# Two layers of a hybrid flow-matching block on one core: a new order for the first products, the sums of squares and the background modulation

## The chip, the cores and the metric

One core of one Trainium2 chip runs the whole program; times are device microseconds (us). A kernel is run several times and the median is compared. Engines in the text: PE is TensorE (matmuls), PEld its weight loads, DVE is VectorE, ACT is ScalarE, POOL is GpSimd, SP is SyncE, on whose queue all the DMAs named here are issued.

## The reference

512 latent tokens and 256 context tokens of width 1024 go through two layers, each a half-step SwiGLU, a mixer, and a second half-step SwiGLU; in each of the three the normalised input is scaled and shifted by a learned modulation of a conditioning vector. Cut to what matters here:

```
mod = (silu(c) @ w_mod[l] + b_mod[l]).reshape(c.shape[0], N_MOD, 1, D_MODEL)     # 9 blocks of 1024 columns
h = rms_norm(x, norm_g[l, 0]) * (1.0 + mod[:, 1]) + mod[:, 0]                     # scale and shift
u = h @ w_in
x = x + 0.5 * mod[:, 2] * ((silu(u[..., :D_FF]) * u[..., D_FF:]) @ w_out)         # D_FF = 2816
...
return rms_norm(x, final_norm_g)
```

The context tokens take the same path with their own modulation vector. The last layer's second SwiGLU has the latent tokens alone.

## The kernel before, in words

Everything is kept transposed in SBUF, as eight tiles `xT[k]` of 128 features by 768 tokens. The four feed-forward passes (`ffn`) loop over 22 steps `ff` of 128 columns of D_FF. A step is one call of `up`, which computes both up-projections of 128 columns by seven half-size products in place of eight (`EVEN1`, `T1`, `T2`, `ODD1`, `T3`, `ODD2`, `T4`). Each product is 4 pairs of feature tiles times 3 matmuls (both operands are split into a high and a low part), 12 matmuls in all, and accumulates in one of three PSUM banks `b`, `c`, `a` (tile name `ul`). The activations of the seven products are the tiles `bh`/`bl` (`self.B`), made on ACT and DVE by `pair_even` and by the generator `pair_odd`; the weights are `w1h`/`w1l`. `EVEN1` goes to `b`, is copied to `p1`, and `T2` and `T4` then add to the same bank; `T1` goes to `c`, is copied to `p5`, and `ODD2` adds to it. After `up` come the multiplication by the row's reciprocal root mean square (`rsb`), silu and gate (tiles `u`, `sg`, then `gh`/`gl`), and every two or three steps a chunk of down-projection (`mm3`, tile `y`), which DVE adds to `xT` (L595).

The RMS normalisation is applied behind the products. Its sums of squares are made by `sumsq(k)`: ACT squares a tile (`sq`), and six PE matmuls of one column each (`ssps`) add it up over the partitions. `raw_rows` turns the sums into reciprocal roots (`ssc`, 12 small DVE instructions) and spreads them over the partitions by six matmuls into two PSUM banks (`rst`).

The modulation is 18 blocks of 512 columns a layer. `mod_direct` and `mod_some` multiply the silu of the conditioning by weights (`wm`, eight loads of 256 KB for a block), `mod_rows` copies the sums (`mrow`) and transposes them by small matmuls (`modpt`) into `mod`. At the head, blocks 8 and 12 (scales of the first pass) and 0 and 4 (its shifts) are made directly. The shifts enter the products as two more columns of the activations (`raw_shifts`); the first `up` is computed without these columns, and a separate product (`bias`, L1102) adds them. The other blocks are made in the background of three `ffn` passes, by halves of four matmuls: 28 halves in the first pass, 12 in the second, 24 in the third. In each step `mod_some` does one half, or two in a row while more halves than steps are left, and loads the next half's four weights behind each.

A planner orders the instructions of each engine by a priority, which is the order of the program shifted by `high_priority(offset)`; a negative offset puts a block that many instructions later. What isn't ready by the planner's clock is passed over. Buffers of one tag are a ring. Tags that matter here:

```
PSUM "u", 7 banks: xps, modps (mod_direct), ul, rst, y, fps     PSUM "ms", 1 bank: modps (mod_some), modpt, ssps, bias
"t3", 2 buffers: sq, mrow, u                                    "wm", 4 buffers: weights of a half
"pc", 4 buffers: p1, p5, u2 (copies of ul), four x2 at the head "wo", 1 buffer: x3, wm6 (six weights of blocks 0 and 4), wb, wo
```

In the first pass `first_mods` makes the scales, the activations for `EVEN1` and then all eight sums of squares with offset -150; `first_shifts`, called behind the first `up`, loads and makes blocks 0 and 4 and the shifts. In the last pass `fin_tile(n)` squares, sums and transposes (`fps`) the finished tile of `xT` directly behind its down-projection, and `finish` normalises and stores.

Of the kernel before, what the change touches and what calls it, by code (L numbers as in the profile page):

```python
# [18 lines left out]
F32 = mybir.dt.float32  # L19
# [9 lines left out]
KT = 8  # L29
# [15 lines left out]
LATER = 300  # L45
SOON = 20
REST = 100
LATE0, LATE4, SQ0, SQ1 = 0, 0, 150, 150
NWQ, NW1, NPC = 6, 4, 4


# [71 lines left out]
class Whole:  # L123
# [103 lines left out]
            for k, r in enumerate(self.mod_w):  # L227
                self.nc.sync.dma_start(out=r, in_=self.a["w_mod"][l, (4 * h + k) * 128:(4 * h + k + 1) * 128, b * 128:b * 128 + 512])

    def mod_some(self, left):  # L230

        nc = self.nc
        for _ in range(2 if len(self.mod_todo) + 1 > left else 1):
            if self.mod_now is None:
                return
            l, b, h = self.mod_now
            if h == 0:
                self.mod_ps = self.psum("modps", "ms")
            for k, r in enumerate(self.mod_w):
                with self.tc.high_priority(offset=k):  # L240
                    nc.tensor.matmul(self.mod_ps[32 * k:32 * k + 32, :], lhsT=self.sc[:, 4 * h + k, :], rhs=r, start=h == 0, stop=h == 1,
                                     skip_group_check=True)
            if h == 1:
                self.mod_rows(l, b, self.mod_ps)
            self.mod_load()

    def scales(self, l, n, v):

# [163 lines left out]
    def ready(self, l, n, segs=SEGS, tag="ms"):  # L412

        def cb(k):
            if k == 0:
                self.raw_open(l, n, segs)
                self.held, self.rest = [], []
            with self.tc.high_priority(offset=-SQ1):
                self.sumsq(k, segs, tag)
            if n == 1:  # L420
                self.raw_tile(k)
                return
            m = k // 2
            if k % 2 == 0:
                self.held.append([self.half_tile() for _ in range(3)])
                self.pair_even(m, segs, self.held[m][0])
                return
            e2, o2, t = self.held[m]
            self.rest.append(self.pair_odd(m, segs, e2, o2, t))
            for _ in range(3):  # L430
                next(self.rest[m])
            if k == KT - 1:
                for i in range(3):
                    with self.tc.high_priority(offset=-REST - 15 * i):
                        for c in self.rest:
                            next(c)
        return cb
# [49 lines left out]
    def up(self, l, i, ff, first):  # L487


        nc, H = self.nc, self.half  # L490
        W = H + 2
        b, c, a = [self.psum("ul", "u") for _ in range(3)]
        ops = self.w1_operands(*(self.first_w1 if first else self.w1_load(l, i, ff)))
        z = 2 if first else 0
        keep = lambda: self.fw.tile([128, W], F32, name="pc", tag="pc", bufs=NPC)

        def product(n, out, start):
            wh, wl = next(ops)
            if first and n != EVEN1:
                for r in self.rest:  # L500
                    next(r, None)
            xh, xl = self.B[n]
            x0 = z if n in SHIFTED else 0
            for m in range(KT // 2):
                for j, (w, x) in enumerate(((wh, xh), (wh, xl), (wl, xh))):
                    nc.tensor.matmul(out, lhsT=w[:, m, :], rhs=x[:, m, x0:], start=start and m == j == 0, stop=m == KT // 2 - 1 and j == 2,  # L506
                                     skip_group_check=True)

        t = self.work.tile([128, 2 * H + 2], F32, name="u2", tag="t3")
        g = self.fw.tile([128, 2 * H], F32, name="sg", tag="sg", bufs=1)  # L510
        add = lambda out, x, y: nc.vector.tensor_tensor(out=out, in0=x, in1=y, op=ALU.add)
        product(EVEN1, b[:, z:W], True)
        p1 = keep()
        nc.scalar.copy(p1[:, z:W], b[:, z:W])
        product(T1, c[:, :H], True)
        p5 = keep()
        nc.scalar.copy(p5[:, :H], c[:, :H])
        product(T2, b[:, z:W], False)
        u2 = keep()
        nc.scalar.copy(u2[:, :H], b[:, 2:W])  # L520
        product(ODD1, a[:, z:W], True)
        add(t[:, z:W], a[:, z:W], p1[:, z:W])
        product(T3, b[:, 2:W], False)
        add(g[:, H:], b[:, 2:W], p5[:, :H])
        product(ODD2, c[:, :H], False)
        add(t[:, W:], c[:, :H], u2[:, :H])
        product(T4, b[:, z:W], False)
        return t, g, b

    def ffn(self, l, i, segs, chunks, background, last_cb, switch):  # L530
        nc, a = self.nc, self.a
        w2 = a["ffn_w_out"]
        H = self.half
        self.mod_todo = [(*t, h) for t in background for h in range(2)]
        f = 0
        for ci, cn in enumerate(chunks):
            gs = []
            for j in range(cn):
# [29 lines left out]
                gs.append((gh, gl))  # L568
                with self.tc.high_priority(offset=-LATER):
                    if ff:  # L570
                        self.mod_some(DFF // 128 - ff)
                    else:
                        self.mod_load()

# [13 lines left out]
            for n_ in range(KT):  # L588
                wh, wl = self.split(wo[:, :, n_ * 128:(n_ + 1) * 128], [128, cn, 128], "w2")
                py = [self.psum("y", "u")[:, :n] for o, n in segs]  # L590
                for j in range(cn):
                    self.mm3(py, wh[:, j, :], wl[:, j, :], gs[j][0], gs[j][1], segs, j == 0, j == cn - 1)
                for s, (o, n) in enumerate(segs):
                    xs = self.xT[n_][:, o:o + n]
                    nc.vector.scalar_tensor_tensor(out=xs, in0=py[s], scalar=gt[s][:, n_:n_ + 1], in1=xs, op0=ALU.mult, op1=ALU.add)  # L595
                if ci == len(chunks) - 1:
                    last_cb(n_)
            f += cn

    def gates(self, l, n, segs, half):  # L600
# [459 lines left out]
    def first_mods(self):  # L1060

        nc = self.nc
        ring = lambda pool, tag, n, bufs: [pool.tile([128, 512], F32, name="wm", tag=tag, bufs=bufs) for _ in range(n)]
        for b in (8, 12):
            self.mod_direct(0, b, self.mod_pieces(0, b, ring(self.hl, "w1h", 4, NW1) + ring(self.hl, "w1l", 4, NW1)))
        self.first_w1 = self.w1_load(0, 0, 0)
        self.raw_open(0, 0, shifts=False)
        self.rest = []
        for m in range(KT // 2):
            x2 = self.hl.tile([128, 2, self.half], F32, name="x2", tag=("gh", "gl")[m % 2], bufs=3)  # L1070
            t = self.fw.tile([128, self.half], F32, name="x2", tag="pc", bufs=NPC)
            self.pair_even(m, SEGS, x2[:, 0, :])
            self.rest.append(self.pair_odd(m, SEGS, x2[:, 0, :], x2[:, 1, :], t))
        for c in self.rest:
            next(c)
        with self.tc.high_priority(offset=-SQ0):
            for k in range(KT):
                self.sumsq(k)
            self.raw_rows(self.fw)

    def first_shifts(self):
        nc = self.nc
        ring = lambda pool, tag, n, bufs: [pool.tile([128, 512], F32, name="wm", tag=tag, bufs=bufs) for _ in range(n)]
        for b, late in ((0, LATE0), (4, LATE4)):
            w = self.raw.tile([128, 6, 512], F32, name="wm6", tag="wo", bufs=1)
            bufs = self.mod_pieces(0, b, [w[:, i, :] for i in range(6)] + ring(self.raw, "wm", 2, 4))
            with self.tc.high_priority(offset=-late):
                self.mod_direct(0, b, bufs, late)
        with self.tc.high_priority(offset=-LATE4 - 10):
            self.raw_shifts(0, 0)  # L1090

            w = self.raw.tile([128, KT, 256], F32, name="wb", tag="wo", bufs=1)
            for u in range(2):
                nc.sync.dma_start(out=w[:, :, 128 * u:128 * u + 128],
                                  in_=self.a["ffn_w_in"][0, 0, :, (1 - u) * DFF:(1 - u) * DFF + 128].rearrange("(k p) n -> p k n", p=128))
            sh = self.fw.tile([128, KT, 2], F32, name="sh0", bufs=1)
            for v in range(2):
                nc.vector.tensor_copy(sh[:, :, v], self.mod[0][v][:, :KT])
            pt = self.psum("bias", "ms")
            for u in range(2):  # L1100
                for k in range(KT):
                    nc.tensor.matmul(pt[:, 2 * u:2 * u + 2], lhsT=w[:, k, 128 * u:128 * u + 128], rhs=sh[:, k, :], start=k == 0, stop=k == KT - 1)  # L1102
            self.bias0 = self.fw.tile([128, 2, 2], F32, name="bias0", bufs=1)
            nc.vector.tensor_copy(self.bias0, pt[:, :4].rearrange("p (u v) -> p u v", u=2))
# [593 lines left out]
```

## Time and profile before

| | us |
|---|---|
| median of 3 runs | 3576.63 (3576.49, 3576.63, 3597.42) |
| profiled execution: its time | 3586.14 |
| profiled execution: its span | 3584.3 |
| PE busy / DVE busy / ACT busy in the span | 3417.7 / 2365.4 / 1533.6 |

The span is the profiled execution from its first to its last instruction; 1.8 us of its time lie around it. A busy PE is one that has a matmul in flight, which says nothing of how fast the matmul is.

### The profile page before, as it was taken

The numbers are of one execution on the slowest core, as the hardware profiler recorded it, in microseconds if no ns is written. First come the engines' busy times: TensorE is split into PE (matmuls) and PEld (weight loads), VectorE is DVE, ScalarE is ACT, GpSimd is POOL, SyncE is SP. The second block draws the span as 40 slices with busy tenths as digits, with TensorE's granted clock in tenths as the row PEclk, the third lists the DMA queues.
The fourth block names the chain that finished last, engine by engine and source line by source line (L and its number), as shares of the span: only waits on it lengthen the run. The fifth ranks groups of instructions, "written<-read, shape, count | busy, mean of one in ns | idle before, by whom it ended". The sixth has DMA issues, their size and how long they took to land. (4 is left out here: it accounts for less than half of the span.)

```text
span 3584.3 us, 60380 instructions
## 1 busy us (share of the span) xinstructions
PE 3417.7 (95%) x23736; PEld 2892.2 (81%) x23736; DVE 2365.4 (66%) x5210; ACT 1533.6 (43%) x3342; POOL 163.9 (5%) x342
## 2 busy tenths in 40 slices
PE   6899999999998999999999999999999989999997
PEld 5787898877776666998999879898888776678996
DVE  4566666545547875676777766666555567878885
ACT  4333333322446653433444424333333557644543
POOL 0000000000003230000000000000000022300000
PEclk7999999999999998999999899999999979999998
DMA  4434323211100002233221333323222100032331
GB/s 156 130 105 127 110 91 118 71 48 43 48 14 1 11 13 80 81 95 121 89 69 53 92 103 104 113 91 118 71 59 55 30 8 11 19 94 88 107 104 50
DMA packets 332941, 267.75 MB, mean 75 GB/s; under 512 B 33748, under 2 KB 281712, under 8 KB 332656
## 3 DMA queue, kind: packets, MB, share of 16 engines
q1 hardware_dynamic: 332656, 263.89, 24.0%
q8 instruction: 187, 3.06, 0.4%
q14 instruction: 98, 0.80, 0.1%
HBM read 261.72 MB, written 2.10 MB: 74 GB/s over the span
## 5 line engine op out<-in xcount | busy, mean ns | idle before, releaser
L506 PE MATMUL ul<-bh,w1h 128*128 128x386 f32 (+3 forms) x2464 | 807.5, 328 | 11.0 <-ACT w1h L455 4.1
L506 PE MATMUL ul<-bh,w1l 128*128 128x386 f32 (+3 forms) x2464 | 800.4, 326 | 2.0 <-DVE w1l L456 2.0
L506 PE MATMUL ul<-bl,w1h 128*128 128x386 f32 (+3 forms) x2464 | 802.1, 326 | 0.0
L455 ACT ACTIVATE w1h<-w1r 128x512 fp32r<-128x512 f32 x528 | 328.3, 631 | 499.8 <-PE ul L506 435.3
L506 PEld LDWEIGHTS ul<-bh,w1h 128*128 128x128 f32 x2464 | 467.9, 190 | 39.0 <-issue 15.4
L456 DVE TENSOR_TENSOR w1l<-w1r,w1h 128x512 fp32r<-128x512 f32 x528 | 359.8, 688 | 187.2 <-ACT w1h L455 182.6
L506 PEld LDWEIGHTS ul<-bl,w1h 128*128 128x128 f32 x2464 | 468.8, 190 | 4.6 <-issue 2.5
L506 PEld LDWEIGHTS ul<-bh,w1l 128*128 128x128 f32 x2464 | 467.2, 190 | 2.7 <-DVE w1l L456 2.5
L595 DVE SCALAR_TENSOR_TENSOR xT<-y,gate,xT 128x512 f32<-128x512 f32 x448 | 267.0, 632 | 209.3 <-PE y L447 207.3
L443 PE MATMUL y<-gh,w2h 128*128 128x512 f32 (+1 forms) x1232 | 348.6, 351 | 6.9 <-ACT gh L566 6.9
L445 PE MATMUL y<-gl,w2h 128*128 128x512 f32 (+1 forms) x1232 | 349.6, 349 | 0.3 <-DVE gl L567 0.2
L447 PE MATMUL y<-gh,w2l 128*128 128x512 f32 (+1 forms) x1232 | 347.2, 348 | 0.5 <-DVE w2l L456 0.4
L455 ACT ACTIVATE w2h<-wo 128x384 fp32r<-128x384 f32 (+1 forms) x256 | 124.7, 495 | 339.8 <-PE y L445 300.3
L443 PE MATMUL pj<-hh,pwh 128*128 128x512 f32 (+2 forms) x864 | 254.5, 348 | 1.8 <-DVE qA L1127 1.8
L447 PE MATMUL pj<-hh,pwl 128*128 128x512 f32 (+2 forms) x864 | 245.9, 342 | 1.2 <-DVE pwl L456 1.2
L445 PE MATMUL pj<-hl,pwh 128*128 128x512 f32 (+2 forms) x864 | 246.6, 342 | 0.0
L443 PEld LDWEIGHTS y<-gh,w2h 128*128 128x128 f32 x1232 | 198.9, 189 | 48.5 <-ACT gh L566 12.7
L447 PEld LDWEIGHTS y<-gh,w2l 128*128 128x128 f32 x1232 | 198.3, 190 | 37.1 <-issue 4.2
L445 PEld LDWEIGHTS y<-gl,w2h 128*128 128x128 f32 x1232 | 199.6, 190 | 32.9 <-DVE gl L567 2.3
L443 PEld LDWEIGHTS pj<-hh,pwh 128*128 128x128 f32 x864 | 150.2, 196 | 27.5 <-issue 7.9
L447 PEld LDWEIGHTS pj<-hh,pwl 128*128 128x128 f32 x864 | 146.7, 195 | 19.6 <-issue 5.1
L445 PEld LDWEIGHTS pj<-hl,pwh 128*128 128x128 f32 x864 | 147.7, 196 | 18.1 <-issue 7.6
(375 smaller groups left out, 5226.2 us busy)
## 6 DMA issues: line engine op xcount, KB each, us to landing
w1r<-in_ffn_w_in_dram SPq DMA_DIRECT2D x352, 256.0 KB
wm<-in_w_mod_dram SPq DMA_DIRECT2D x288, 256.0 KB
wo<-in_ffn_w_out_dram SPq DMA_DIRECT2D x88, 512.0 KB
pw<-in_w_in_dram SPq DMA_DIRECT2D x46, 512.0 KB
pw<-in_w_in_dram SPq DMA_DIRECT2D x16, 256.0 KB
wo<-in_w_out_dram SPq DMA_DIRECT2D x128, 32.0 KB
wo<-in_w_out_dram SPq DMA_DIRECT2D x64, 64.0 KB
rtab<-in_k_rope_dram SPq DMA_DIRECT2D x4, 512.0 KB
```

Of the source, the lines that this page charges most:

```text
L443: nc.tensor.matmul(p, lhsT=wh, rhs=xh[:, o:o + n], start=first, stop=False)
L445: nc.tensor.matmul(p, lhsT=wh, rhs=xl[:, o:o + n], start=False, stop=False)
L447: nc.tensor.matmul(p, lhsT=wl, rhs=xh[:, o:o + n], start=False, stop=last)
L455: nc.scalar.activation(out=hi, in_=raw, func=AF.Copy)
L456: nc.vector.tensor_tensor(out=lo, in0=raw, in1=hi, op=ALU.subtract)
L506: nc.tensor.matmul(out, lhsT=w[:, m, :], rhs=x[:, m, x0:], start=start and m == j == 0, stop=m == KT // 2 - 1 and j == 2, skip_group_check ...
L595: nc.vector.scalar_tensor_tensor(out=xs, in0=py[s], scalar=gt[s][:, n_:n_ + 1], in1=xs, op0=ALU.mult, op1=ALU.add)
```

## The change

At the head, the sums of squares leave `first_mods`. They are now called inside the first `up`: tiles 0 to 3 ahead of product `T3`, tiles 4 to 7 ahead of `ODD2`, and `raw_rows` ahead of `T4`, all without an offset. Modulation block 0 is computed ahead of `T1` and block 4 ahead of `ODD1`; the loads of block 0 stand behind those of the first step's weights. `first_shifts` keeps the shifts and the bias, 20 instructions later than its place. In the `ffn` passes `mod_some` does one half only, and a second half is done inside `up`, between `T2` and `ODD1` and without an offset, while the halves left are at least as many as the steps. In the last pass the work of `fin_tile(n)` stands behind the down-projection of tile n + 1.

```
-LATE0, LATE4, SQ0, SQ1 = 0, 0, 150, 150
...
-    def mod_some(self, left):
...
-        for _ in range(2 if len(self.mod_todo) + 1 > left else 1):
-            if self.mod_now is None:
-                return
-            l, b, h = self.mod_now
...
+    def mod_some(self):
+
+        nc = self.nc
+        if self.mod_now is None:
+            return
+        l, b, h = self.mod_now
...
             if first and n != EVEN1:
                 for r in self.rest:
                     next(r, None)
+                if n == T1:
+                    self.mod_direct(0, 0, self.first_w0)
+                    self.first_w4 = self.first_weights(4)
+                if n == ODD1:
+                    self.mod_direct(0, 4, self.first_w4)
+                if n in (T3, ODD2):
+                    for k in range(4):
+                        self.sumsq(k + (4 if n == ODD2 else 0))
+                if n == T4:
+                    self.raw_rows(self.fw)
...
         u2 = keep()
         nc.scalar.copy(u2[:, :H], b[:, 2:W])
+        if len(self.mod_todo) >= DFF // 128 - ff:
+            self.mod_some()
         product(ODD1, a[:, z:W], True)
...
                     if ff:
-                        self.mod_some(DFF // 128 - ff)
+                        self.mod_some()
                     else:
                         self.mod_load()
...
-                    last_cb(n_)
+                    if switch is None and last_cb == self.fin_tile:
+
+                        if n_:
+                            last_cb(n_ - 1)
+                        if n_ == KT - 1:
+                            last_cb(n_)
+                    else:
+                        last_cb(n_)
...
         self.first_w1 = self.w1_load(0, 0, 0)
+        self.first_w0 = self.first_weights(0)
...
-        with self.tc.high_priority(offset=-SQ0):
-            for k in range(KT):
-                self.sumsq(k)
-            self.raw_rows(self.fw)
+
+    def first_weights(self, b):
+        w = self.raw.tile([128, 6, 512], F32, name="wm6", tag="wo", bufs=1)
+        return self.mod_pieces(0, b, [w[:, i, :] for i in range(6)] + [self.raw.tile([128, 512], F32, name="wm", tag="wm", bufs=4) for _ in range(2)])
 
     def first_shifts(self):
-        nc = self.nc
-        ring = lambda pool, tag, n, bufs: [pool.tile([128, 512], F32, name="wm", tag=tag, bufs=bufs) for _ in range(n)]
-        for b, late in ((0, LATE0), (4, LATE4)):
-            w = self.raw.tile([128, 6, 512], F32, name="wm6", tag="wo", bufs=1)
-            bufs = self.mod_pieces(0, b, [w[:, i, :] for i in range(6)] + ring(self.raw, "wm", 2, 4))
-            with self.tc.high_priority(offset=-late):
-                self.mod_direct(0, b, bufs, late)
-        with self.tc.high_priority(offset=-LATE4 - 10):
+
+        nc = self.nc
+        with self.tc.high_priority(offset=-SOON):
             self.raw_shifts(0, 0)
```

## Rows read from the trace of the kernel before

**Rows 1.** The page, busy time of the span, by engine.

```profile
PE 3417.7 (95%) x23736; PEld 2892.2 (81%) x23736; DVE 2365.4 (66%) x5210; ACT 1533.6 (43%) x3342; POOL 163.9 (5%) x342
```

**Rows 2.** Waits of PE, whole run: us in total, times, longest.

```profile
PE modpt L216 <- ACT mrow L213: 18.3, 25, 1.1
PE modps L241 <- DMA wm<-in_w_mod_dram: 17.5, 7, 3.1
PE ssps L265 <- ACT sq L263: 14.3, 3, 12.2
...
PE fps L1625 <- DVE xT L595: 6.8, 8, 0.8
```

**Rows 3.** Waits of the weight loads (PEld), whole run.

```profile
PEld modps L241 <- DMA wm<-in_w_mod_dram: 37.2, 26, 4.0
```

**Rows 4.** Windows of the head: us, busy by engine, PEclk (1.00 is full), DMA share, GB/s.

```profile
0.00:34.00 34.00, 20.37 (x109) 12.76 (x110) 9.51 (x42) 10.37 (x33) 0.20 (x4) 1.00 0.85 284
34.00:70.00 36.00, 21.13 (x100) 20.96 (x100) 13.56 (x34) 18.03 (x37) 0.00 (x0) 0.50 0.19 66
...
50.00:60.00 10.00, 10.00 (x49) 10.00 (x48) 0.00 (x0) 3.13 (x5) 0.00 (x0) 0.50 0.00 0
```

**Rows 5.** Timeline of the head: start, us, engine, line, names, [idle before, releaser].

```profile
33.01 1.50 PE L265 MATMUL ssps<-mean,sq 128*128 128x1 f32 x12 [0.41 <-DVE gs L252]
...
37.27 0.62 DVE L347 SCALAR_TENSOR_TENSOR bl<-xT,gs,bh 128x384 fp32r<-128x384 f32 x1 [0.57 <-ACT bh L346]
...
46.71 18.08 PE L265 MATMUL ssps<-mean,sq 128*128 128x1 f32 x84 [12.20 <-ACT sq L263]
...
49.53 0.84 ACT L263 ACTIVATE sq<-xT 128x768 f32<-128x768 f32 x1 [2.14 <-PE ssps L265]
...
64.83 0.17 DVE L269 COPY ssc<-ssps 128x6 f32<-128x6 f32 x1 [17.10 <-PE ssps L265]
...
67.47 2.50 PE L302 MATMUL rst<-ident,rsr 128*128 128x128 f32 x10 [2.67 <-DVE rsr L286]
69.62 0.67 PE L506 MATMUL ul<-bh,w1h 128*128 128x384 f32 x1
...
83.38 2.73 SPq L196 DMA_DIRECT2D wm<-in_w_mod_dram  x6
...
86.12 1.04 PE L206 MATMUL modps<-wm,sc 128*32 128x512 f32 x2 [0.58 <-DMA wm<-in_w_mod_dram]
...
87.65 3.62 PE L206 MATMUL modps<-wm,sc 128*32 128x512 f32 x14
...
100.60 2.16 PE L1102 MATMUL bias<-sh,wb 128*128 128x2 f32 x18 [0.82 <-PE modpt L216]
102.62 0.99 PE L506 MATMUL ul<-bh,w1h 128*128 128x386 f32 x2
```

**Rows 6.** Groups of the head, 0 to 110 us: busy us, mean ns, idle before.

```profile
L344 DVE TENSOR_TENSOR bl<-x,bh 128x384 fp32r<-128x384 f32 x20 | 10.2, 552 | 8.3 <-ACT bh L343 8.3
```

**Rows 7.** Timeline of one double half of the modulation, first pass.

```profile
147.93 1.07 PE L241 MATMUL modps<-wm,sc 128*32 128x512 f32 x8
149.00 7.10 SPq L228 DMA_DIRECT2D wm<-in_w_mod_dram  x8
151.80 1.75 PE L241 MATMUL modps<-wm,sc 128*32 128x512 f32 x4 [2.81 <-DMA wm<-in_w_mod_dram]
...
154.05 1.69 PE L241 MATMUL modps<-wm,sc 128*32 128x512 f32 x4 [0.50 <-DMA wm<-in_w_mod_dram]
```

**Rows 8.** Timeline of the tail, PE: the transposes of four of eight tiles.

```profile
3534.92 0.66 PE L1625 MATMUL fps<-ident,xT 128*128 128x128 f32 x4 [0.85 <-DVE xT L595]
...
3541.01 0.66 PE L1625 MATMUL fps<-ident,xT 128*128 128x128 f32 x4 [0.85 <-DVE xT L595]
...
3545.52 0.66 PE L1625 MATMUL fps<-ident,xT 128*128 128x128 f32 x4 [0.85 <-DVE xT L595]
...
3570.91 0.66 PE L1625 MATMUL fps<-ident,xT 128*128 128x128 f32 x4 [0.84 <-DVE xT L595]
```

More of the change, by code (lines that the diff above doesn't have):

```diff
@@ L228, in mod_load @@
                 self.nc.sync.dma_start(out=r, in_=self.a["w_mod"][l, (4 * h + k) * 128:(4 * h + k + 1) * 128, b * 128:b * 128 + 512])
-    def mod_some(self, left):
+    def mod_some(self):
         nc = self.nc
-        for _ in range(2 if len(self.mod_todo) + 1 > left else 1):
-            if self.mod_now is None:
-                return
-            l, b, h = self.mod_now
[L237 to L245, printed above, removed]
+        if self.mod_now is None:
+            return
+        l, b, h = self.mod_now
+        if h == 0:
+            self.mod_ps = self.psum("modps", "ms")
+        for k, r in enumerate(self.mod_w):
+            with self.tc.high_priority(offset=k):
+                nc.tensor.matmul(self.mod_ps[32 * k:32 * k + 32, :], lhsT=self.sc[:, 4 * h + k, :], rhs=r, start=h == 0, stop=h == 1,
+                                 skip_group_check=True)
+        if h == 1:
+            self.mod_rows(l, b, self.mod_ps)
+        self.mod_load()
     def scales(self, l, n, v):
@@ L417, in cb @@
                 self.held, self.rest = [], []
-            with self.tc.high_priority(offset=-SQ1):
+            with self.tc.high_priority(offset=-150):
                 self.sumsq(k, segs, tag)
@@ L533, in ffn @@
         H = self.half
+        self.mod_now = None
         self.mod_todo = [(*t, h) for t in background for h in range(2)]
```

## The prediction

> **What bounds the kernel now.** The page comes first: PE is busy for 95% of the span, DVE for 66%, ACT for 43% [rows 1]. So time can be taken out where PE stands still, or where it is busy and slow. The waits of PE name the stalls [rows 2]; the waits of the weight loads say how long the array had nothing to load, also where a matmul still in flight hides that from the first list [rows 3]. Three places of the change appear there: the sums of squares waiting for ACT (12.2 us, once), the background modulation waiting for its weights (17.5 us for PE, 37.2 us for the loads), the transposes of the last pass waiting for DVE (6.8 us). The windows of the head then show the slow work: the clock is full until 34 us, 0.50 from 34 to 70 us, and 0.50 still from 50 to 60 us, where PE is busy all ten microseconds with the one-column matmuls of the sums [rows 4]. The timelines of the three places give the terms [rows 5, 7, 8].
>
> **The head: why the first products come late.** The last operand of `EVEN1` is done at 37.9 us (37.27 + 0.62), and its first matmul runs at 69.62 us, right behind the first spreads `rst` [rows 5]. Nothing it reads is late. What it writes is: `rst` and `ul` are buffers of the one ring "u", `rst` stands earlier in the program, and the product starts as soon as both `rst` banks are taken. I read from this that a ring is handed out in the order in which the program first uses its buffers, whatever the priorities, so the offset of -150 could not let the products pass. The change moves `rst` behind the products in the program, and that frees them.
>
> **The head: the new chain, worked out.** `EVEN1` follows its operands: 37.9 us and 2 to 4 us of matmuls, say 40. Block 0 needs about 2 us of PE behind that (estimate), and only then is the buffer "wo" free for block 4. From the first issue of block 4's loads to its last matmul was 7.9 us (83.38 to 87.65 + 3.62) [rows 5]; so 42 + 8 = 50, and some 2 us for copy, transposes and addition. `ODD1` writes a bank that the ring gives out behind block 4's; its activations come behind those of three `T1` and three `T2` pairs on DVE, about 0.55 us an instruction [rows 6], which with the weights' parts also ends near 50. Its 12 matmuls and the addition into `u` bring 53 us.
>
> The sums come behind that, and they have lost a buffer: squares, `mrow` and `u` share the two buffers of "t3", and before the change all squares stood ahead of the first `u` in the program. Now `u` is taken first and kept to the end of the step, so one buffer is left, and each tile's square, handover, sums and handover go one after the other: 0.84 + 0.2 + s + 0.2 us, where s is 1.50 us at full clock (12 records at 33.01) and 2.58 us at half clock (18.08 x 12 / 84) [rows 5]. Eight tiles take 8 x 2.74 = 22 us or 8 x 3.82 = 31 us, to 75 or 84 us. From `ssc` to the first spread are 2.6 us (64.83 to 67.47) and to the first product behind it 2.2 more (69.62): the second step's products start at 80 or 89 us, where they start at 102.62 now. Before that point 2.16 us of the bias had run; after the change it has to wait for the "ms" bank until the sums are done, so 2 us come back. The head gives 20 or 12 us. I take 15, nearer to half clock, since the sums ran at 0.50 where they were dense [rows 4]. The other products (`T3`, `ODD2`, `T4`) run in the gaps of the sums and cost nothing of their own; if the gaps are cold, that is in the 12. `raw_shifts` and the bias load are off this chain: their cover is the same 22 to 31 us of sums.
>
> The sums are small matmuls behind large weight loads. The Trainium skill, TensorE: Matmul & The Clock Gate, section LDWEIGHTS (loading the stationary operand), gives 128 columns / 1.2 = 107 ns for a load and no clock in it. By that the twelve loads of a tile would take 1.28 us at either clock, the eight tiles 20 us, and the head would give 22 us in place of 15. The rows above say 125 ns at full and 215 ns at half clock, and I go by them.
>
> **The background modulation.** Before, a step that has two halves to do puts them back to back, and the second half's loads wait for the first half's matmuls, since the four "wm" buffers are all there are. One such place: first half 147.93 us, 1.07 us; loads issued from 149.00; second half from 151.80, done at 155.74 [rows 7]. It ended 6.7 us behind the first where 1.07 would do: 5.7 us lost. PE stood like this 7 times (17.5 us), and the whole loss is the loads' 37.2 us [rows 2, 3]. By the counting rule of the kernel there are ten double steps, seven in the first pass (28 halves for 21 steps) and three in the third (24); the second pass has no double.
>
> The change does not take a matmul away. It puts the first half of each pair inside `up`, between `T2` and `ODD1`; the second half stays at the end of the step, with its offset of -300. The pair's second half then finds its weights loaded. What may be lost again: the first half's weights are issued behind the half before it, and it has a priority above ready products. Behind it on PE are queued the four products from `ODD1` on, and behind these DVE's additions. If the planner's clock is right it is passed over until its weights are there. I price a misjudgement at 1 us for each of ten halves, by the nearest wait of a modulation matmul that a planner's misjudgement leaves, `modpt` for `mrow` with 0.73 us on average and 1.1 at most [rows 2]. That leaves 37 - 10 = 27 us. The bounds are 37, if all ten are covered, and a loss of 20, if all ten stand for a full 5.7 us (57 against 37). SP's queue is also better off: eight weight loads that waited for matmuls held it for 7.10 us [rows 7], with the step's own loads behind them; now they go in fours. I cost that at nothing, and its cover is that the step's loads are issued a step ahead. The wait of `modpt` for `mrow` (18.3 us) stays, since there is still one copy for each block.
>
> **The tail.** From the first transpose to the last are 36.0 us for seven tiles, 5.14 us each; the fastest gap is 4.51 us [rows 8]. In each PE stands 0.85 us for the addition to `xT`, since the next tile's banks come behind `fps` in the ring "u" [rows 2, 8]. With `fin_tile` one tile later the next down-projection covers it, and only the last tile's wait is left: 7 x 0.85 = 6 us. The slow gaps are worth another 7 x (5.14 - 4.51) = 4.4 us if they go as well. I take 8, between 6 and 10.
>
> **The sum.** 15 + 27 + 8 = 50 us. Against the profiled execution that is 3586.14 - 50 = 3536 us. The profiled execution is 9.5 us above the median, so for the median I forecast 3576.6 - 50 = 3527 us.
>
> **The rivals.**
> Early halves that wait: the weights come later than the planner thinks, and the middle gives 5 us in place of 27. For it speaks that a half's loads need some 6 us behind the half before [rows 7]; against it that PE is passed on to other products while the planner knows of the wait. Time: 15 + 5 + 8 = 28 us, 3549 us.
> The sums eat the head: one buffer, half clock, and block 4 later than I think by ten microseconds, because its loads queue on SP behind others. The head gives 0, the rest stays: 35 us, 3542 us.
> Slower: early halves stand on PE ahead of ready products, with SP's queue held by other waiting loads (7.10 us) ahead of their own (6.7 us): 14 us each at most, 10 taken. Ten cost 100 us against 37 saved, and with 23 us from head and tail the kernel is 40 us slower, 3617 us. It decides from 6 us a half, (37 + 23) / 10. Against it: the weights of the next half are issued as soon as a buffer is free, half a step ahead.
> The change doesn't do what it says: the planner's order of the first pass comes out as before, since its clock and not the program's order decides, and only the tail is gained: 3569 us.
>
> **How the numbers follow.** The forecast 0.60, waiting halves 0.17, a head without gain 0.13, slower 0.05, no new order 0.05. The range reaches from all upper ends together (20 + 42 + 10 = 72, with 5 us for `modpt` waits that denser work covers: 3505 us) to the waiting halves with the lower ends of head and tail (12 + 5 + 6 = 23: 3554 us); what it leaves out is slower, no new order, and some of the rest. One per cent, about what a measurement of this kernel can tell from no change, is 36 us: below 3541 us. Nearly all of the forecast lies there, half of the case without a head and a little of the waiting halves: 0.65 faster, 0.30 within, 0.05 slower.
>
> **What would show it.** In the profile after: the first `ul` near 38 us, not 70; squares with PE's `ssps` as releaser ahead of seven of them, at a period of 2.7 to 3.8 us, and the second step's products (386 columns) at 80 to 89 us; the granted clock there, 0.50 or more. The loads' wait for "wm" from 37.2 to 10 us or less. The last pass with transposes 3.5 to 4 us apart and no wait for DVE but the last. The prediction is wrong if the loads' wait stays above 25 us, or moves to other names (`mrow`, `gh`), if the second step starts later than 95 us, or if PE gains new stalls in the steps between 110 and 670 us or 2040 and 2560 us that no part above names.

## The result, and the profile after

The changed kernel takes 3540.86 us (median of 4 runs, 3535.18 to 3546.41); the kernel before, on the same chip, 3578.7 us. The ratio is 0.9889, with a 95% interval from 0.9852 to 0.9927. That is some 40 us less (26 to 53), where 50 were forecast. The time lies in the forecast's range, and 0.1 us below the line of 3541 us, which is closer than these runs can tell; the three parts gave other amounts than the terms of the sum. The profiled execution has a span of 3543.5 us, 40.8 us less than the one before.

The page's busy line, and the waits of PE and of the weight loads, whole run, of the changed kernel:

```profile
PE 3406.4 (96%) x23736; PEld 2874.4 (81%) x23736; DVE 2365.9 (67%) x5210; ACT 1532.2 (43%) x3342; POOL 162.5 (5%) x342
```

```profile
PE modpt L215 <- ACT mrow L212: 18.8, 24, 1.3
...
PE ssps L263 <- ACT sq L261: 7.4, 8, 1.7
...
PEld ul L514 <- issue: 40.5, 51, 1.5
```

Against [rows 1 to 3]: the wait of the background matmuls for their weights (17.5 us for PE, 37.2 us for the loads) is gone from both lists, and so is `fps` behind `xT`, but for 0.4 us. The sums still wait for ACT, 7.4 us in eight pieces in place of 14.3. PE is busy 11.3 us less, although the change takes no matmul away; where matmuls became cheaper or dearer this net figure doesn't say.

One wait of the loads has grown. "Issue" is idle time for which the profile shows no releaser; in front of the products it is now 40.5 us (last line above), where it was in the kernel before:

```profile
PEld ul L506 <- issue: 17.9, 25, 0.8
```

Windows of the head, changed kernel (us, PE busy, granted clock, DMA share, GB/s), to be held against [rows 4]:

```profile
34.00:50.00 16.00, 12.93 (x36) 0.73 0.49 171
50.00:60.00 10.00, 10.00 (x33) 0.75 0.36 118
60.00:70.00 10.00, 8.64 (x60) 0.93 0.84 266
70.00:90.00 20.00, 17.41 (x74) 0.50 0.00 0
90.00:100.00 10.00, 9.46 (x43) 0.71 0.10 28
100.00:110.00 10.00, 9.75 (x56) 0.83 0.60 210
```

The slow stretch of [rows 4], 34 to 70 us, has not gone: it has moved behind the first four products (48 of 84 matmuls), to 70 to 90 us, where PE is busy 87% of the time and the granted clock is 0.50. Timelines of the head in the changed kernel, against [rows 5]:

```profile
34.69 0.69 PE L514 MATMUL ul<-bh,w1h 128*128 128x384 f32 x1 [1.16 <-ACT bh L344]
...
58.06 1.06 PE L205 MATMUL modps<-wm,sc 128*32 128x512 f32 x6
...
65.90 1.50 PE L263 MATMUL ssps<-mean,sq 128*128 128x1 f32 x12 [0.99 <-ACT sq L261]
...
79.41 2.72 PE L263 MATMUL ssps<-mean,sq 128*128 128x1 f32 x12 [0.99 <-ACT sq L261]
...
98.80 3.71 PE L1116 MATMUL bias<-sh,wb 128*128 128x2 f32 x32 [0.54 <-issue]
102.76 1.92 PE L239 MATMUL modps<-wm,sc 128*32 128x512 f32 x2 [0.25 <-DVE bias L1118]
104.61 2.31 PE L300 MATMUL rst<-ident,rsr 128*128 128x128 f32 x12
106.67 0.42 PE L514 MATMUL ul<-bh,w1h 128*128 128x386 f32 x1
```

```profile
90.04 0.16 DVE L267 COPY ssc<-ssps 128x6 f32<-128x6 f32 x1 [1.88 <-PE ssps L263]
...
94.88 0.16 DVE L275 TENSOR_SCALAR rsv<-ssc 128x6 f32<-128x6 f32 x1
...
103.30 0.16 DVE L284 SCALAR_TENSOR_TENSOR rsr<-rsb,rsr 128x6 f32<-128x6 f32 x1
```

The first product is at 34.69 us (forecast near 38). The second step's first product of 386 columns is at 106.67 us, where [rows 5] have 102.62 and 80 to 89 were forecast. The first down-projection `y` is at 147.88 us, before at 145.75. By these two traces the head lost 2 us. That is no more than two traces of one head differ by: `tail_only` below, whose head is that of the kernel before, has its first `y` at 148.28 us. So nothing was gained, and a loss isn't shown.

A place of two halves in the first pass, and the transposes of the last pass, changed kernel (against [rows 7, 8]):

```profile
150.06 1.07 PE L239 MATMUL modps<-wm,sc 128*32 128x512 f32 x8
...
154.92 1.05 PE L239 MATMUL modps<-wm,sc 128*32 128x512 f32 x4
...
156.79 1.05 PE L239 MATMUL modps<-wm,sc 128*32 128x512 f32 x2
...
158.73 1.04 PE L239 MATMUL modps<-wm,sc 128*32 128x512 f32 x2
```

```profile
3515.63 0.63 PE L1639 MATMUL fps<-ident,xT 128*128 128x128 f32 x4
...
3518.96 0.64 PE L1639 MATMUL fps<-ident,xT 128*128 128x128 f32 x4
...
3529.02 1.07 PE L1639 MATMUL fps<-ident,xT 128*128 128x128 f32 x8
```

No half waits any more. But the half inside `up` runs in three pieces between other matmuls, and a piece of two records (one of the four matmuls) takes 1.04 us where all eight records together take 1.07. Behind a piece the next weight load stands idle, here behind the first of the three:

```profile
155.90 0.19 PEld L514 LDWEIGHTS ul<-bl,w1h 128*128 128x128 f32 x1 [0.84 <-issue]
```

The transposes shown are 3.33 us apart (5.14 on average before). From the first to the last they take 21.5 us in place of 36.0.

### The profile page after: what moved, and what is told of

The parts are those of the page before. It is cut to its first block, busy times and chain, and to the rows that moved or that the text cites. A ratio compares the mean times of both kernels' runs of the same rounds, so it can differ in the third digit from the quotient of the medians.

```text
span 3543.5 us, 60390 instructions
## 1 busy us (share of the span) xinstructions
PE 3406.4 (96%) x23736; PEld 2874.4 (81%) x23736; DVE 2365.9 (67%) x5210; ACT 1532.2 (43%) x3342; POOL 162.5 (5%) x342
## 5 line engine op out<-in xcount | busy, mean ns | idle before, releaser
L514 PEld LDWEIGHTS ul<-bl,w1h 128*128 128x128 f32 x2464 | 468.7, 190 | 14.2 <-issue 10.8
L443 PE MATMUL y<-gl,w2h 128*128 128x512 f32 x1232 | 347.3, 347 | 0.1
L445 PE MATMUL y<-gh,w2l 128*128 128x512 f32 x1232 | 345.1, 347 | 0.5 <-DVE w2l L454 0.4
```

The lines of the kernel that those rows point to most:

```text
L443: nc.tensor.matmul(p, lhsT=wh, rhs=xl[:, o:o + n], start=False, stop=False)
L445: nc.tensor.matmul(p, lhsT=wl, rhs=xh[:, o:o + n], start=False, stop=last)
```

## The experiments

**The three parts alone.** Each is the kernel before with one part of the change and nothing of the others; of each edit a few lines are shown.

```diff
@@ head_only: up(), first step
+                if n == T1:
+                    self.mod_direct(0, 0, self.first_w0)
...
@@ mods_only: up()
+        if len(self.mod_todo) >= DFF // 128 - ff:
+            self.mod_some()
         product(ODD1, a[:, z:W], True)
...
@@ tail_only: the last pass's last chunk
+                        if n_:
+                            last_cb(n_ - 1)
...
```

> The kernel before with the head's part of the change alone. By the prediction the head alone gives 12 to 20 us: the second step's first product of 386 columns at 80 to 89 us, and a time of some 3562 us. By the trace of the changed kernel it gives nothing: that product stood at 106.67 us there, 4 us later than before, and the first y at 147.9 us, 2 us later; so the first y comes at 145 to 149 us here and the time is 0 to 4 us above the kernel before.

Ratio 0.9993 (0.9978 to 1.0007): 2.5 us, not to be told from none. First product of 386 columns at 103.93 us, first `y` at 143.94. The forecast's 12 to 20 us are excluded.

> The kernel before with the halves of the background modulation at two places of a step, and nothing else. By the prediction 27 us less (between 37 less and 20 more). By offsets between the two traces, 20 to 27 us less: 12 in the first pass, 13 in the third. If the two other parts are needed for it (an order of the planner that only comes out with the new head), less than 10 us. The rival of early halves that wait gives 5 us.

Ratio 0.9955 (0.9938 to 0.9971): 16 us less (10 to 22); by the offset of the second mixer in the trace 21. It doesn't need the other parts. The loss to waiting halves (5 us left) is excluded, and so are the full 27 us. Half of the loads' 37.2 us is back under another name:

```profile
PEld ul L505 <- issue: 36.4, 47, 0.8
```

That is 18.5 us more than before, and 42 of the 47 waits stand directly behind a piece of `modps`. In front of `modps` itself "issue" grew by 4.3 us (14.2 to 18.5). What is left of the 37.2 us is some 14, about what the run measured.

> The kernel before with the last pass's transposes one tile later, and nothing else. By the prediction 8 us less (6 to 10); by the offsets between the two traces 14 us less, with transposes 3.3 us apart in place of 5.1. If part of the 14 us belongs to the clock in the changed kernel and not to the delay, the gaps stay above 4 us and 6 to 10 us are gained.

Ratio 0.9959 (0.9943 to 0.9974): 15 us less (9 to 20), and the last `y` is 14.3 us earlier. Transposes are 3.35 us apart here too:

```profile
3542.74 0.63 PE L1632 MATMUL fps<-ident,xT 128*128 128x128 f32 x4
...
3546.09 0.64 PE L1632 MATMUL fps<-ident,xT 128*128 128x128 f32 x4
```

The three add up to 33 us, within the interval of the whole change. Where the rest of the tail's gain comes from is in the windows of the kernel before and of this one (columns as above):

```profile
3530.00:3540.00 10.00, 7.39 (x29) 0.83 0.01 2
3540.00:3550.00 10.00, 7.57 (x43) 1.00 0.00 0
3550.00:3560.00 10.00, 8.67 (x42) 0.84 0.00 0
3560.00:3570.00 10.00, 8.69 (x42) 0.84 0.01 2
```

```profile
3530.00:3540.00 10.00, 9.44 (x52) 1.00 0.01 2
3540.00:3550.00 10.00, 10.00 (x65) 1.00 0.00 0
```

Before, PE stood for a quarter to an eighth of each stretch, and the granted clock was 0.83 or 0.84 in three of the four; with the waits gone PE is busy nearly throughout and the clock is 1.00.

**What a piece costs.** The changed kernel; `packed_halves` has both edits, `whole_halves` the first alone, `split_early` the second alone; two hunks that only fit other places to the one tile of four weights are left out.

```diff
-            self.mod_w = [self.raw.tile([128, 512], F32, name="wm", tag="wm", bufs=4) for _ in range(4)]
+            w = self.raw.tile([128, 4, 512], F32, name="wm", tag="wm", bufs=1)
+            self.nc.sync.dma_start(out=w, in_=self.a["w_mod"][l, 4 * h * 128:(4 * h + 4) * 128, b * 128:b * 128 + 512].rearrange("(k p) n -> p k n", p=128))
+            self.mod_w = [w[:, k, :] for k in range(4)]
...
-                with self.tc.high_priority(offset=k):
+                with self.tc.high_priority(offset=LATER + 60 + k):
```

> The changed kernel, with the four weights of a half loaded by one transfer and its four matmuls put directly behind one another in the order of PE: 76 runs of modulation matmuls in place of 101. If each separate run costs 1.05 us however few of the four column groups are in it, as 8 records in 1.06 us and 2 records in 1.04 us say, 25 fewer runs give 20 to 26 us less than the changed kernel, 3515 to 3521 us. If the short runs lie beside other work, or if the halves now wait for their one large transfer, the time is within 5 us of the changed kernel or above it.

Median 3516.13 us, ratio 0.9825 (0.9806 to 0.9845): 25 us below the changed kernel, as expected.

> The changed kernel with one transfer for the four weights of a half and the priorities as they were: 88 runs of modulation matmuls in PE's order in place of 101, the transposes still directly behind them. By 1.05 us a run 13 us less than the changed kernel, PE's busy time with them 99 us less 13, and the wait for the copied row still at 18 us. If the one large transfer has its price in waits (14 us in the packed kernel), it is the priority that exposes it, and here it stays below 5 us; else the time is that of the changed kernel.

Median 3534.05 us, ratio 0.9877 (0.9847 to 0.9907). That is 7 us less than the changed kernel by the medians (13 expected), and the intervals overlap, so the time alone doesn't show a gain. The span of the profiled execution is 17.4 us shorter, but it is the fastest of its four runs.

> The changed kernel (four transfers a half, as there) with only the priority of the packed kernel: the modulation matmuls ahead of ready products, 114 separate runs of them in PE's order in place of 101 (packed: 76), and the transposes of the rows no longer directly behind the matmuls. If what counts is the number of runs at 1.05 us each, PE's busy time with modulation matmuls rises from 99 us to some 110 us; the wait for the copied row goes as in the packed kernel (18.8 to some 2 us), so the time is within 6 us of the changed kernel. If the packed kernel's gain came from the priority alone, this one has it too: 20 us or more below the changed kernel.

Median 3556.92 us, ratio 0.9941 (0.9917 to 0.9966): 16 us above the changed kernel, 10 us outside what was expected. The groups by line of the background's matmuls and of the transposes of rows (busy us, mean ns, idle before), for the changed kernel, `whole_halves`, `packed_halves` and `split_early` in turn:

```profile
L239 PE MATMUL modps<-wm,sc 128*32 128x512 f32 x512 | 99.0, 608 | 0.5 <-DVE bias L1118 0.3 <-DMA wm<-in_w_mod_dram 0.2
L215 PE MATMUL modpt<-pick,mrow 128*128 128x2 f32 x288 | 38.7, 255 | 18.8 <-ACT mrow L212 18.8
```

```profile
L239 PE MATMUL modps<-wm,sc 128*32 128x512 f32 x512 | 82.3, 608 | 4.1 <-DMA wm<-in_w_mod_dram 3.7 <-DVE bias L1119 0.3
L215 PE MATMUL modpt<-pick,mrow 128*128 128x2 f32 x288 | 37.5, 252 | 17.2 <-ACT mrow L212 17.2
```

```profile
L239 PE MATMUL modps<-wm,sc 128*32 128x512 f32 x512 | 72.0, 621 | 18.1 <-DMA wm<-in_w_mod_dram 14.3 <-issue 3.1 <-PE modpt L215 0.4
L215 PE MATMUL modpt<-pick,mrow 128*128 128x2 f32 x288 | 38.1, 239 | 2.4 <-ACT mrow L212 2.4
```

```profile
L239 PE MATMUL modps<-wm,sc 128*32 128x512 f32 x512 | 127.0, 618 | 9.0 <-DMA wm<-in_w_mod_dram 5.4 <-issue 3.1 <-DVE bias L1118 0.3
L215 PE MATMUL modpt<-pick,mrow 128*128 128x2 f32 x288 | 36.8, 230 | 2.0 <-ACT mrow L212 2.0
```

The same 512 records, with nearly the same mean duration, keep PE busy for 72.0, 82.3, 99.0 or 127.0 us, in the order of the pieces, unbroken runs in PE's order, that they are cut into: 64, 76, 90 and 103. (The 76, 88, 101 and 114 expected count the 11 or 12 pieces of the head's direct blocks too.) From 64 to 90 pieces that is 27.0 / 26 = 1.04 us each, the duration of one piece. In the changed kernel a piece of two records takes 1.11 us on average and one of eight 1.09. Of the 26 pieces, 14 go with the one transfer (`whole_halves`) and 12 only with the priority besides. The last step is larger, 28.0 us for 13 pieces: `split_early` has 17 pieces of four records, which take 1.90 us on average. In them the two matmuls stand behind one another (records start at 313.76, 314.22, 314.45 and 314.90 us); side by side, as in the changed kernel, they start in pairs (154.92, 154.92, 155.37, 155.38) and take 1.05. That is some 14 us more, and 13 pieces at 1.05 us are the other 14. The mean duration of a record says nothing of it, because it doesn't tell whether four of them overlap.

The second column of reading is the idle time. `packed_halves` gains 27.0 us by fewer pieces and 16.4 by the copied row (18.8 to 2.4: its transposes no longer stand directly behind the matmuls), and gives back 17.6 us (0.5 to 18.1), most of it waits for the one large transfer (14.3): 25.8 us in sum, against 26.0 us of span. `split_early` has the same 16.8 us from the row and pays 28.0 and 8.5, a loss of 19.7 us by this account, where its span is 12.4 us longer and its median 16; so the account is good to some 7 us. The priority alone is no gain, and with the packing it is.

The Trainium skill, TensorE: Matmul & The Clock Gate, section Part 3: Packing small matmuls — row/col tiling, gives the time of a pack as one matmul's duration and about 4 ns for each further tile. The trace agrees where the four stand together (1.07 us against 1.04 for one).

**The head.** Three edits of the changed kernel, each aimed at one reason why its chain came out late; of each edit a few lines are shown. By the first `y` of a single trace, differences up to the 2.5 us between the two like heads above say nothing.

```diff
@@ own_squares
+                        self.sumsq(k + (4 if n == ODD2 else 0), sq=self.hl.tile([128, T], F32, name="sq", tag=("gh", "gl")[k % 2], bufs=3))
@@ own_copies
+        p1 = self.hl.tile([128, W], F32, name="pc", tag="gh", bufs=3) if first else keep()
+        two = self.hl.tile([128, 2 * H], F32, name="pc", tag="gl", bufs=3) if first else None
+        p5 = two[:, :H] if first else keep()
+        u2 = two[:, H:] if first else keep()
@@ head_packed
+        for i, n in ((0, 4), (4, 2)):
+            self.nc.sync.dma_start(out=w[:, i:i + n, :], in_=rows(i, n).rearrange("(k p) n -> p k n", p=128))
```

> The changed kernel with the head's squares in two free buffers of another ring in place of the one left of t3. By the prediction's chain (square 0.84, handovers 0.4, sums 1.5 or 2.6 us, one after the other), two buffers leave only the sums: a period of 1.5 us at full clock and 2.7 us at half clock in place of 2.5 and 3.7, 8 to 9 us earlier at the first spread, and the first y at 139 to 141 us in place of 147.9. If ACT, which has the activations of the last pairs between the squares, is the limit, the period stays above 3 us and 0 to 3 us are gained.

Ratio 0.9877 (0.9849 to 0.9905). The last sums start at 82.02 us in place of 87.45, 5.4 earlier, but the first spread `rst` is only 3.8 us earlier (100.79, where 8 to 9 were expected), the first product of 386 columns 3.3 (103.37) and the first `y` 2.5 (145.35). That lies in the band given to a limit by ACT, but here no sum of the head waits for a square any more. PE takes up the room at once; windows of this kernel (busy of PE, PEld, DVE, ACT and POOL, then the granted clock):

```profile
70.00:80.00 10.00, 10.00 (x45) 10.00 (x45) 7.02 (x14) 4.62 (x9) 0.00 (x0) 0.50 0.01 2
80.00:90.00 10.00, 10.00 (x45) 10.00 (x45) 5.24 (x13) 4.75 (x15) 0.00 (x0) 0.60 0.09 26
```

> The changed kernel with the first step's three copies of partial products in free buffers of another ring, so that they no longer wait for the last operands of the first step. Then the products T3 and ODD2 can run in the gaps of the sums, as the prediction had it, and the reciprocal root behind the sums is not spread over 13 us by additions that wait for them. If that was what ate the head's gain: the second step's first product 10 to 14 us earlier than 106.67, the first y at 135 to 139 us. If the sums' own period (3.7 us at half clock) sets the end, 3 to 5 us.

Ratio 0.9894 (0.9861 to 0.9927), first product of 386 columns at 106.03 us, first `y` at 147.98: nothing. The products do run between the sums now, and the last sums start 2.8 us later for it (90.21). That the products came behind the sums instead of into their gaps was not the price.

> The changed kernel with the first six weights of the head's blocks 0 and 4 loaded by two transfers in place of six, so that their matmuls become ready together: 2 and 4 separate runs of them in PE's order in place of 4 and 5. Between 20 us and the first y, PE spends 23.7 us on modulation matmuls in the changed kernel, where it spent 16.2 before. If single runs are the price here as in the steps, three fewer at 1.05 us (full clock) to 1.9 us (half clock) give 3 to 6 us: the first y at 142 to 145 us in place of 147.9, the time 3 to 6 us lower. If something else sets the head's end, the first y stays within 1 us.

Ratio 0.9902 (0.9888 to 0.9916), first `y` at 148.23 us: nothing. The two blocks take 19.3 us in place of 21.4, so the cut was small, and it didn't reach the first `y`.

Then the sums themselves, left out for seven of eight tiles:

```diff
-                    for k in range(4):
-                        self.sumsq(k + (4 if n == ODD2 else 0))
+                    if n == ODD2:
+                        self.sumsq(0, only=True)
```

> The changed kernel without the squares and sums of seven of the head's eight tiles (the sums of the first tile alone are taken). If the head is bound by PE's own work, of which the sums at half clock are 18.3 us with 9.7 us of stalls, and the products between them run at half clock for their sake (6 us more than before), the first y comes 20 to 27 us earlier, at 121 to 128 us. If the sums lie beside waiting that is there anyway (the weights, the operands of T4), less than 8 us are gained.

Ratio 0.9828 (0.9814 to 0.9842): 24 us below the changed kernel; the first `y` at 131.45 us, 16.4 earlier, where 20 to 27 were expected. The sums' own time on PE (17.5 us for seven tiles) shows almost whole, so they lie beside no waiting. This run takes the chain of squares away with PE's work; what tells the two apart is `own_squares`, which shortens the chain and leaves the work. What didn't come is the rest: the products between them stay slow, and the granted clock without the sums is still 0.63 from 70 to 80 us, where PE now stands a third of the time:

```profile
70.00:80.00 10.00, 6.56 (x26) 6.08 (x27) 9.55 (x31) 3.22 (x8) 0.00 (x0) 0.63 0.10 28
```

**Together.** Whole halves, squares in their own buffers and the blocks' fewer transfers; in `all_three`, where `off` is 0 inside `up` and LATER behind the step; `all_three_root` also has the reciprocal root and its spreads ahead and the bias later.

```diff
@@ all_three
-                with self.tc.high_priority(offset=k):
+                with self.tc.high_priority(offset=off + k):
@@ all_three_root
+                    with self.tc.high_priority(offset=60):
+                        self.raw_rows(self.fw)
...
-        with self.tc.high_priority(offset=-SOON):
+        with self.tc.high_priority(offset=-150):
             self.raw_shifts(0, 0)
```

> Whole halves kept together (the early half at its own place, the late one at the priority of its place), squares in their own buffers and the head's blocks by fewer transfers. 24.7 us below the changed kernel for the packed halves, 2.5 for the squares, 3 to 6 for the blocks, and up to 5 of the 14 us that the packed halves wait for their transfer, since the late half comes later: 3504 to 3512 us.

Median 3508.06 us, ratio 0.9806 (0.9787 to 0.9825): in the expected span, and below both kernels. The waits for the large transfer fell only from 14.3 to 12.1 us; the first `y` is at 143.9 us, with one more background half and 24 more product matmuls ahead of it. The second step starts at 97.27 us, 9.4 earlier than in the changed kernel: up to the first `y` the blocks' matmuls take 17.0 us in place of 21.4, the sums 17.5 in place of 19.0, and PE's idle time is 7.0 us in place of 9.8, 8.7 us together.

> The same, and the reciprocal root put ahead of the additions on DVE and of the bias (the bias by then 150 later). If PE's work bounds the head, its first y is within 2 us of the kernel without this and the time within 3 us; if the root's chain, spread over 13 us in the changed kernel, sets the end, the first y comes 6 to 10 us earlier.

Median 3509.08 us, ratio 0.9800 (0.9785 to 0.9815): the same. The spreads come 2.2 us earlier (92.89), the first `y` 2.9 us later (146.79), a little outside the 2 us given for a head that PE's work bounds and far from the 6 to 10 us earlier of the other case. The chain of the root doesn't set the head's end, as far as an edit that moved it by 2.2 us can show.

## Why the prediction was right or wrong

**The head: wrong, 15 us forecast, none measured.** The reason for the late first products was right: the first `ul` moved from 69.62 to 34.69 us once `rst` stood behind it in the program. The period of the sums was right too (2.5 us at full clock and 3.7 at half, forecast 2.7 and 3.8), and so was that there is one buffer left. Three steps failed, and the sign named for it came: the second step starts later than 95 us. Block 4 was done at 59 us, not 50, and the first sums ran at 63.41, not behind 53: its matmuls and block 0's went one by one between the products of `EVEN1` and `T1`, at half clock in part. "The other products (`T3`, `ODD2`, `T4`) run in the gaps of the sums and cost nothing of their own" was false: 36 matmuls (12 for each) start mostly behind 85 us, at 0.32 us each while the clock is half. And from `ssc` to the first spread passed 14.6 us (90.04 to 104.61), not 2.6: DVE did the additions of the late products between the root's twelve instructions, and PE these products, the bias and a background half. (The 0.2 us of a handover, for which the prediction shows no row, was under 0.1: 0.99 us stood between two tiles' sums, 0.84 of them the square.) The step behind all three is that I followed a chain of waits and put the work of PE at nothing. The groups of PE between 20 us and the first `y`, kernel before and then after:

```profile
L506 PE MATMUL ul<-bh,w1h 128*128 128x384 f32 (+1 forms) x104 | 36.7, 357 | 2.6 <-ACT bh L343 1.4 <-ACT pc L517 1.2
...
L265 PE MATMUL ssps<-mean,sq 128*128 128x1 f32 x96 | 19.6, 340 | 12.6 <-ACT sq L263 12.2 <-DVE gs L252 0.4
L206 PE MATMUL modps<-wm,sc 128*32 128x512 f32 x64 | 16.4, 603 | 0.7 <-DMA wm<-in_w_mod_dram 0.7
```

```profile
L514 PE MATMUL ul<-bh,w1h 128*128 128x384 f32 (+1 forms) x104 | 38.9, 374 | 1.7 <-ACT bh L344 1.2 <-ACT bh L341 0.5
...
L205 PE MATMUL modps<-wm,sc 128*32 128x512 f32 x64 | 21.4, 678 | 2.0 <-DMA wm<-in_w_mod_dram 2.0
L263 PE MATMUL ssps<-mean,sq 128*128 128x1 f32 x96 | 19.0, 325 | 4.0 <-ACT sq L261 3.8
...
L239 PE MATMUL modps<-wm,sc 128*32 128x512 f32 x8 | 3.0, 719 | 0.3 <-DVE bias L1118 0.3
```

PE's idle time there fell from 21.0 to 9.8 us, 11.2 us gained. The same work took longer: 5.0 us for the two blocks, 6.0 us for the products (from one start to the next, all three kinds, 58.9 to 64.9), and 3.0 us for a background half that now stands ahead of the first `y`. 14.0 against 11.2 is the 2 to 3 us between these two traces. The runs bear it out from the other side: shortening the chain (`own_squares`, `own_copies`, `all_three_root`) moves the first `y` by 3 us or less either way, taking PE work away moves it by nearly all of that work (`one_tile_sums`) and moves the second step by what PE saves (`all_three`). Of the rivals, "the sums eat the head" named the amount (0) and block 4's ten microseconds; its one buffer is worth 2.5 us at most.

The Trainium skill's rule for weight loads that is weighed there (TensorE: Matmul & The Clock Gate, section LDWEIGHTS (loading the stationary operand): 107 ns, no clock in it) is borne out at full clock alone. In the kernel after the twelve loads of a tile start 112 ns apart at a granted clock of 1.00 and 213 ns apart at 0.50. The prediction's 125 ns is the whole 1.50 us of a tile divided by twelve, with the end of the last matmul in it; at half clock a tile took 2.72 us, near its 2.58.

**The background modulation: 27 us forecast, 16 to 21 measured; the mechanism right, one term mis-sized.** The 37.2 us of the loads' waits are gone under their name, but in `mods_only` 18.5 of them stand again in front of the products and 4.3 in front of `modps`. A move to other names is one of the prediction's signs of being wrong (it has `mrow` and `gh` in mind); half of the wait did so, to "issue". The ten us taken off for misjudged halves were put on the wrong thing, a wait of each early half for something late. None waits. The planner places the four matmuls of a half one by one, in part as their weights come in, and each piece costs a whole 1.05 us, in which the loads behind it stand: `packed_halves` shows 27 us of PE's time in it. The halves that waited before were cut as well (100.6 us busy before, 99.0 after), so the waits' end brought no better packing with it. The wait of `modpt` for `mrow` stayed, as forecast (18.3 and 18.8 us).

**The tail: 8 us forecast, 15 measured.** The step that was mis-sized is the slow gaps, put at 4.4 us "if they go as well" and taken at two. They went: with the stalls of 0.85 us went the half clock between them too (the windows above), and the remaining gap is 3.33 us, not the 4.51 - 0.85 = 3.66 that the fastest gap before promised. From the first transpose to the last 14.5 us are saved (36.0 to 21.5), of which the waits for `xT` are 6.4 (6.8 to 0.4).

**The sum.** 50 us were forecast as 15 + 27 + 8; the parts alone measured 2 + 16 + 15 = 33, the whole change 40, with 13 us of uncertainty. That it lies in the range owes much to the tail, which made up for half of what the head didn't give. The rival "the sums eat the head" gave 3542 us, nearer than the forecast's 3527, but with 27 and 8 for the other two parts; that its sum fits is luck too.

## What to carry to other kernels

Before a chain of waits is shortened, add up what the bound engine has to do in that stretch, at the clock it will have: where PE is busy anyway, an earlier start only moves the slow work. Matmuls that share the array by column groups belong in one uninterrupted run; let their operands become ready together, and watch the group's busy time, not the mean of one. A stall on PE is priced with the clock behind it, read from windows on both sides.

## What was not expected of the hardware

A full engine did not bring the clock up: in `own_squares` PE and its weight loads are busy for all of 70 to 80 us, mostly with one-column matmuls, and the granted clock there is 0.50, the lower of its two levels (1.2 GHz). And in the last pass, where PE stood 0.85 us at each transpose, three of four windows show 0.83 or 0.84, so stretches at half clock; without these waits it is 1.00. The fourth window before shows 1.00 too, although PE is busy for only 7.57 of its 10 us.
